# Experts in threes of 32 slots, with 32 slots more that a TensorE register assigns, and weights in tiles of three places

## The chip, the cores and the metric

The kernel runs on one core of one Trainium2 chip. The metric is the device time of one execution in microseconds (us); shorter is better.

## The reference

Two networks run one after the other on 256 tokens of 1024 numbers in float32. The first mixes tokens, attends to a memory and has a dense feed-forward part. The second has two layers, each a token mixer and then a mixture of 32 experts, both steered by numbers (`mod`) computed from a condition `c` with the weights `w_ada`. Only the mixture is touched by the change:

```python
for layer in range(DEPTH_2):
    mod = c_act @ w_ada[layer] + b_ada[layer]
    sh_mix, sc_mix, g_mix, sh_ffn, sc_ffn, g_ffn = jnp.split(mod[:, None, :], 6, axis=-1)
    ...
    x = x + (g_mix * mixed).astype(x.dtype)
    h = (rmsnorm(x, norm_ffn_g[layer]) * (1.0 + sc_ffn) + sh_ffn).astype(x.dtype)
    moe = hierarchical_moe(h, ...)
    x = x + (g_ffn * moe).astype(x.dtype)
...
# in hierarchical_moe: 4 groups of 8 experts; the best group, and in it the best 2
weights = jax.nn.softmax(top_logit, axis=-1) * p_grp
expert_id = g_idx[:, None] * EXPERTS_PER_GROUP + top_idx
combine = ...
hid = jax.nn.silu(jnp.einsum('td,edf->tef', t, w_gate[sl])) * jnp.einsum('td,edf->tef', t, w_up[sl])
y = y + jnp.einsum('tef,efd->td', hid * combine[:, sl, None], w_down[sl])
```

A token uses 2 of the 32 experts. An expert has gate and up weights of 1024 x 256 and down weights of 256 x 1024, 1 MiB each, so a layer's experts hold 96 MiB. Counted from the reference's inputs, no expert of layer 0 has more than 25 tokens; in layer 1 expert 5 has 35 and all others at most 26.

## The kernel before

Everything is kept on the chip except the weights, which stream in through one queue: SyncE issues every weight transfer in program order, and a transfer waits there until its place is free. A place is 8 KB a partition and takes one tile `w` of 128 x 2048 numbers, 1 MiB. The places come from pools (`wst` 5, `wst2` 2, `wst3` 5, later 3, `wst4` 3); `load_w` (L208 in the profile) takes the next place in turn. Matrix products outside the experts split both operands in two parts and take three products (`mm3`, L261 to L263).

The `ada` weights are used by a filler: its tiles (L1031) and matmuls (L1033, four groups of 32 columns that write to different partitions of a bank) are put among other work. Behind each third of a layer's `mod`, four transposes (L1045) bring it into columns.

A mixture begins when the mixer's last residual sum is made (L1188 multiplies by the gate row, L1189 adds). Then come the norm, transposes (`to_T`, L362), router logits (L1631), `route` (L1520 to L1567), which gives each token's rank within its expert (`rankm`) and its weight (`comb`), and the main loop of 16 steps `j` of two experts with 64 slots each:

- `group(G)`, once for two steps: one-hot matrices `Sg` of tokens by slots (L1655), and with them the gather by matmul (L1667), which gives the slots' transposed activations `XT`; the slots' weights `cslot` (L1682).
- `gate(j)` and `up(j)`: `pair_mm` (L1574), eight slices of 128 of the 1024 inputs, each with a matmul of 64 columns for the one expert and one for the other.
- `mid(j)`: transposes of the product into `hd`, and of `Sg` into `ST` (L1706, L1709, copies at L1712, L1714).
- `down(j)`: L1723, output 512 wide, scaled and split into `oh`, `ol` (L1729 to L1731).
- `scatter(j)`: L1738 and L1739 add the slots back to tokens in four banks `yb`.

A float32 matmul shows as two records on TensorE, a transpose as one. TensorE's order in the loop is written by hand: gate j, down j-1, up j, scatter j-1, a piece of gather, mid j, a piece of gather. The weights arrive in the order gate j, down j-1, up j (`ExpertLoads`, seven pairs asked for ahead). Gate and up tiles are read with row k x 128 + p on partition p, so their runs in memory are 1 KB; the down tiles' are 4 KB, and ada's 8 KB. If an expert had more than 64 tokens, a branch (`overflow`) would compute the rest; with these inputs it doesn't run.

Of the kernel before, what the change touches and what calls it, by code (L numbers as in the profile page):

```python
# [9 lines left out]
F32 = mybir.dt.float32  # L10
F32R = mybir.dt.float32r
# [14 lines left out]
for _name, _w in (("g_mix_pre", 8), ("conv_w", 16), ("conv_b", 4), ("lru_b_a", 4), ("lru_b_x", 4),  # L26
# [67 lines left out]
def _params(a):  # L94
# [9 lines left out]
    for name in ("g_mix_pre", "conv_w", "conv_b", "lru_b_a", "lru_b_x", "lru_a_param", "pool_scale",  # L104
                 "b_gate", "g_mem_pre", "g_mem_kv", "g_ffn_pre", "norm_mix_g_2", "norm_ffn_g_2",
                 "conv_w_2", "conv_b_2", "ssd_norm_g_2", "hgrn_norm_g_2", "hgrn_lower_bounds_2", "c_2", "b_ada_2"):
        put(name, cols(a[name]))
    put("ssd_d_2", cols(np.repeat(a["ssd_d_2"], 64, axis=1)))
# [23 lines left out]
class Net:  # L132
# [4 lines left out]
    def __init__(self, ctx, tc, A, out, dbg=None, stop=None):  # L137
# [3 lines left out]
        self.cap = 64  # L141
# [46 lines left out]
    def wtile(self):  # L188

        place = self.places.pop(0)  # L190
        self.places.append(place)
        return place[0].tile([P, 2048], F32, name="w", tag=place[1])

# [10 lines left out]
    def load_w(self, src, k, n):  # L204

        t = self.wtile()
        v = t[:, :k * n].rearrange("p (k n) -> p k n", k=k)
        self.nc.sync.dma_start(v, src.rearrange("(k p) n -> p k n", p=P))  # L208
        return v
# [194 lines left out]
    def build(self):  # L404
# [4 lines left out]
        self.kept = [self.more_places(ctx, "wst", 5)]  # L409
# [51 lines left out]
    def mixer1(self, ph):  # L461
# [121 lines left out]
        self.kept.append(self.more_places(self.ctx, "wst2", 2))  # L583
# [426 lines left out]
    def ada(self):  # L1010
# [9 lines left out]
        for l in range(2):  # L1020
# [6 lines left out]
            for g in range(3):  # L1027
# [16 lines left out]
                for c in range(4):  # L1044
# [3 lines left out]
                                cols(self.V["b_ada_2"], l * 48), op=OP.add)  # L1048
                self.ready = 3 * l + g
# [18 lines left out]
    def mixer2(self, l):  # L1068
# [5 lines left out]
        with c:  # L1074
# [435 lines left out]
    def route(self, l, pr, lg, comb, rankm, cnt):  # L1510
# [24 lines left out]
        o2, M = T("o2", 32), T("Mx", 32)  # L1535
        for tt in range(2):
            v.tensor_scalar(o2[:, tt], iota[:, :32], ei[:, tt, 1:2], None, op0=OP.is_equal)
        for tt in range(2):
            v.scalar_tensor_tensor(M[:, tt], iota[:, :32], ei[:, tt, 0:1], o2[:, tt], op0=OP.is_equal, op1=OP.add)
        bk = self.bank()  # L1540
        te.matmul(bk[:, 0:64], C["before"], M.rearrange("p t e -> p (t e)"), start=True, stop=False)
        te.matmul(bk[:, 32:64], C["ones"], M[:, 0], start=False, stop=True)
        v.scalar_tensor_tensor(rankm, bk[:, 0:64].rearrange("p (t e) -> p t e", t=2), 1.0, M, op0=OP.add, op1=OP.mult)
        v.tensor_scalar(rankm, rankm, -1.0, None, op0=OP.add)
# [6 lines left out]
        w1, w2 = T("w1", 1), T("w2", 1)  # L1551
# [6 lines left out]
        for tt in range(2):  # L1558
            v.tensor_scalar(t[:, tt], iota[:, :32], ei[:, tt, 0:1], w1[:, tt], op0=OP.is_equal, op1=OP.mult)
# [304 lines left out]
```

## Time and profile before

| | |
|---|---|
| median of 3 runs | 1407.7 us (1407.28 to 1409.37) |
| profiled execution | 1404.32 us, span 1402.5 us |
| TensorE matmuls busy | 1320.0 us, 94% of the span |
| VectorE, ScalarE busy | 731.3 us (52%), 571.7 us (41%) |
| weight queue (q1) | 367.84 MB, 77.3% of 16 engines' span |
| mean granted clock | 0.980 |

The span runs from the first to the last instruction of the one execution that was profiled; the profiled execution's own time is a little longer than its span. A busy share is a mean over stages: the experts of the two layers take about 709 to 959 and 1143 to 1391 us of the span.

### The profile page before, as it was taken

How to read it: one execution, taken by the hardware profiler on the slowest of the kernel's cores; microseconds unless marked ns; L12 is line 12 of the kernel's file. 1: busy time of each engine (PE TensorE's matmuls, PEld its weight loads, DVE VectorE, ACT ScalarE, POOL GpSimd, SP SyncE). 2: the span in 40 equal slices, each digit the busy share in tenths (PEclk: the TensorE clock that was granted, in tenths of full speed). 3: DMA queues.
4: the chain of work that ended last, by engine and by line, in shares of the span. 5: the costliest groups of instructions: out<-in, count | busy, mean ns of one | idle time of the engine just before them, and what ended most of it. 6: DMA issues, size and time to landing. Idle time of an engine off the chain costs nothing. (4 is left out here: it accounts for less than half of the span.)

```text
span 1402.5 us, 23768 instructions
## 1 busy us (share of the span) xinstructions
PE 1320.0 (94%) x9842; PEld 1040.5 (74%) x9842; DVE 731.3 (52%) x1350; ACT 571.7 (41%) x1056; POOL 86.1 (6%) x95
## 2 busy tenths in 40 slices
PE   7999999999999998999799999988999989999995
PEld 7988898966999976888666666556888666666652
DVE  5797656536555546865533333326766543333323
ACT  5577546545444435465322222215455322222122
POOL 2000000000000002211100000002121110000000
PEclk9998999999999999999899999998999979999998
DMA  9542559689965539653799999998663499999995
GB/s 309 176 158 92 165 180 317 239 342 366 327 189 200 182 128 327 209 181 121 280 310 366 366 366 366 366 373 305 211 211 121 153 331 366 366 366 367 367 366 188
DMA packets 254817, 375.75 MB, mean 268 GB/s; under 512 B 7057, under 2 KB 221201, under 8 KB 248305
## 3 DMA queue, kind: packets, MB, share of 16 engines
q1 hardware_dynamic: 252960, 367.84, 77.3%
q0 software_dynamic: 1312, 5.21, 1.1%
q8 instruction: 79, 1.29, 0.4%
q10 hardware_dynamic: 432, 1.13, 0.2%
q14 instruction: 34, 0.27, 0.1%
HBM read 373.11 MB, written 1.05 MB: 267 GB/s over the span
## 5 line engine op out<-in xcount | busy, mean ns | idle before, releaser
L225 DVE TENSOR_TENSOR wlo<-w,whi 128x1024 fp32r<-128x1024 f32 x214 | 263.0, 1231 | 181.4 <-ACT whi L223 181.0
L223 ACT ACTIVATE whi<-w 128x1024 fp32r<-128x1024 f32 x214 | 226.4, 1060 | 254.4 <-PE bk L262 171.2
L261 PE MATMUL bk<-hTh,whi 128*128 128x256 f32 (+1 forms) x1128 | 321.0, 287 | 0.8 <-ACT whi L223 0.7
L262 PE MATMUL bk<-hTl,whi 128*128 128x256 f32 (+1 forms) x1128 | 316.4, 281 | 2.1 <-DVE hTl L368 1.9
L263 PE MATMUL bk<-hTh,wlo 128*128 128x256 f32 (+1 forms) x1128 | 315.3, 281 | 0.1
L1574 PE MATMUL bk<-w,XT 128*64 128x256 f32 x2048 | 238.5, 381 | 13.3 <-DMA w<-in_w_up 13.3
L261 PEld LDWEIGHTS bk<-hTh,whi 128*128 128x128 f32 (+1 forms) x1128 | 210.9, 188 | 15.2 <-issue 4.1
L1574 PEld LDWEIGHTS bk<-w,XT 128*64 128x64 f32 x2048 | 146.2, 137 | 100.2 <-DMA w<-in_w_up 16.9
L262 PEld LDWEIGHTS bk<-hTl,whi 128*128 128x128 f32 (+1 forms) x1128 | 210.2, 186 | 4.8 <-DVE hTl L368 2.5
L263 PEld LDWEIGHTS bk<-hTh,wlo 128*128 128x128 f32 (+1 forms) x1128 | 210.0, 186 | 0.7 <-DVE wlo L225 0.3
L1723 PE MATMUL bk<-w,hd 128*64 128x512 f32 x512 | 117.5, 593 | 2.1 <-DMA w<-in_w_down 1.2
L1730 ACT ACTIVATE oh<-od 128x512 fp32r<-128x512 f32 x64 | 40.3, 629 | 116.4 <-DVE od L1729 116.4
L1723 PEld LDWEIGHTS bk<-w,hd 128*64 128x64 f32 x512 | 36.9, 137 | 63.3 <-issue 54.8
L1712 ACT ACTIVATE hd<-bk 128x256 f32<-128x256 f32 x32 | 12.3, 385 | 174.1 <-PE bk L1709 174.1
L1675 DVE TENSOR_SCALAR XT<-bk,ga,modcol 128x256 f32<-128x256 f32 x64 | 34.8, 544 | 85.0 <-PE bk L1667 81.8
L1695 DVE SCALAR_TENSOR_TENSOR mth<-mth,bk 128x256 f32<-128x256 f32 x32 | 13.5, 421 | 118.8 <-ACT mth L1694 118.8
L1731 DVE TENSOR_TENSOR ol<-od,oh 128x512 fp32r<-128x512 f32 x64 | 44.3, 692 | 46.8 <-ACT oh L1730 46.6
L1667 PE MATMUL bk<-Sg,xh 128*128 128x256 f32 x256 | 66.8, 294 | 1.3 <-DVE Sg L1655 1.3
L1667 PE MATMUL bk<-Sg,xl 128*128 128x256 f32 x256 | 64.3, 286 | 0.0
L1729 DVE TENSOR_TENSOR od<-bk,gb 128x512 f32<-128x512 f32 x64 | 44.0, 688 | 37.7 <-PE bk L1723 37.7
L1738 PE MATMUL yb<-oh,ST 128*128 128x512 f32 x128 | 54.4, 425 | 1.6 <-ACT oh L1730 1.6
L1667 PEld LDWEIGHTS bk<-Sg,xh 128*128 128x128 f32 x256 | 49.5, 194 | 4.6 <-issue 2.0
(496 smaller groups left out, 2056.8 us busy)
## 6 DMA issues: line engine op xcount, KB each, us to landing
w<-in_w_gate SPq DMA_DIRECT2D x64, 1024.0 KB, 12.0
w<-in_w_up SPq DMA_DIRECT2D x64, 1024.0 KB, 13.2
w<-in_w_down SPq DMA_DIRECT2D x64, 1024.0 KB, 11.2
w<-in_w_in SPq DMA_DIRECT2D x48, 1024.0 KB, 6.2
w<-in_w_ada SPq DMA_DIRECT2D x48, 1024.0 KB, 5.1
w<-in_w_ffn_in SPq DMA_DIRECT2D x22, 1024.0 KB, 11.5
w<-in_w_out SPq DMA_DIRECT2D x12, 1024.0 KB, 5.1
w<-in_w_ffn_out SPq DMA_DIRECT2D x11, 1024.0 KB, 10.1
```

Source lines behind the costliest of these rows:

```text
L223: self.nc.scalar.activation(W.hi, v, AF.Copy)
L225: self.nc.vector.tensor_tensor(W.lo, v, W.hi, op=OP.subtract)
L261: mm(out, l.hi, r.hi, start=start, stop=False)
L262: mm(out, l.hi, r.lo, start=False, stop=False)
L263: mm(out, l.lo, r.hi, start=False, stop=stop)
L1574: self.nc.tensor.matmul(out[i * 64:i * 64 + 64, :S], XT[:, k, c0:c0 + 64], w[i][:, k, :], start=k == 0, stop=k == KT - 1)
L1667: te.matmul(o, xx[:, tt, d * P:(d + 1) * P], Sg[:, tt].rearrange("p e r -> p (e r)"), start=n == 0, stop=n == 3)
L1723: te.matmul(bks[h][i * 64:i * 64 + 64, :], hd[:, f, i * 64:i * 64 + 64], wd[i][:, f, h * 512:h * 512 + 512], start=f == 0, stop=f == 1)
L1729: v.tensor_tensor(t, bks[h], self.gb[:, h * 512:h * 512 + 512], op=OP.mult)
L1730: act.activation(o.hi, t, AF.Copy)
L1731: v.tensor_tensor(o.lo, t, o.hi, op=OP.subtract)
L1738: te.matmul(yb[tt][h], ST[:, tt * P:(tt + 1) * P], os[h].hi, start=j == 0, stop=False)
```

## The change

The experts are taken in threes, in eleven steps (the last has two). A step has 128 slots in four groups of 32: groups 1 to 3 belong to the three experts, and group 0 to the first of the three that was chosen more than 32 times, for its tokens from rank 32 on. Which one that is is known only at run time: `route` writes eleven indices to `idx`, they are loaded to TensorE's registers ahead of the loop (L1825), and group 0's matmul reads the third of the weight tile that the register names. `slots_mm` (L1621) takes the place of `pair_mm`: four matmuls of 32 columns for each slice. The branch for overfull experts now acts on what is left above 32, or 64 for the expert with the spare slots; with these inputs it doesn't run.

All expert tiles are read with rows p x 8 + k (down: p x 2 + f) on partition p, which makes each partition's part one run of 8 KB; the columns of `XT` and of the transposed product are permuted to fit, by strided copies into `xh`, `xl` and by a permuted copy of `mod` and of the norm's factors. That copy is made by sixteen matmuls with one column behind the transposes of the second and third part of each layer's `mod` (L1073).

The weights' places are now a ring of five tiles with three places each, 15 MiB as before. The ring is opened when the mixture begins, after the places of before are closed (`self.top`, `self.wctx`); layer 0 closes it again and opens the old places for the mixer of layer 1.

```diff
-    def load_w(self, src, k, n):
+    def load_w(self, src, k, n, rows="(k p)"):
...
+                if g:
+                    bk = self.bank()
+                    twin = row.rearrange("p (i k) -> p k i", k=8)
+                    for k in range(8):
+                        for h in range(2):
+                            q = (2, 0)[g - 1] + h
+                            te.matmul(bk[h * 64:h * 64 + 64, k:k + 1], twin[:, k], self.ident[:, q * 32:q * 32 + 1],
+                                      start=True, stop=True)
...
-            old, self.places = self.places, []
-            self.more_places(self.top, "wst3", 3)
-            self.places[:0] = old
...
+        v.tensor_scalar(over, count, 32.0, None, op0=OP.is_gt)
+        v.tensor_copy(sel[:, :, 0], over[:, :, 0])
+        v.tensor_tensor(sel[:, :, 1], over[:, :, 1], over[:, :, 0], op=OP.is_gt)
+        v.tensor_tensor(both, over[:, :, 0], over[:, :, 1], op=OP.max)
+        v.tensor_tensor(sel[:, :, 2], over[:, :, 2], both, op=OP.is_gt)
+        v.scalar_tensor_tensor(idx[:, :11], sel[:, :, 2], 2.0, sel[:, :, 1], op0=OP.mult, op1=OP.add)
...
         for k in range(KT):
-            for i in range(2):
-                c0 = j * P + i * 64
-                self.nc.tensor.matmul(out[i * 64:i * 64 + 64, :S], XT[:, k, c0:c0 + 64], w[i][:, k, :],
+            for i in range(4):
+                c0 = j * P + i * 32
+                wi = w[i]
+                self.nc.tensor.matmul(out[i * 32:i * 32 + 32, :S], XT[:, k, c0:c0 + 32], wi[:, k * S:(k + 1) * S],
                                       start=k == 0, stop=k == KT - 1)
...
-                k, n = (2, D) if name == "w_down_2" else (KT, S)
-                self.ready.append([self.net.load_w(self.net.A[name][self.l, 2 * j + i], k, n) for i in range(2)])
+                t = self.net.wtiles(True)
+                for i in range(min(3, 32 - 3 * j)):
+                    self.net.nc.sync.dma_start(t[:, i], self.net.A[name][self.l, 3 * j + i].rearrange("(p k) n -> p (k n)", p=P))
+                self.ready.append(t)
...
+            self.top.close()
+            self.wctx.close()
+            rp = (c, self.ctx)[l].enter_context(tc.tile_pool(name="ring", bufs=1, side="right", reuse_waits="tile"))
+            self.ring = [(rp, "t%d" % i) for i in range(5)]
...
+            def weights(j):
+                w = loads.get()
+                return [w[:, bass.ds(ats[j], 1)].rearrange("p o n -> p (o n)")] + [w[:, i] for i in (0, 1, min(2, 31 - 3 * j))]
...
+            _, ats = nc.values_load_multi_w_load_instructions(
+                idx[0:1, :11], engines=[mybir.EngineType.PE], min_val=0, max_val=2,
+                skip_runtime_bounds_check_because="idx is 2 a + b of two flags of which at most one is set")
```

Two places show how instructions move. The first is SyncE's queue where layer 0's mixture begins. Before, expert tiles stand among the mixer's output weights and ahead of three of the four ada tiles:

```order
L208 DMA w<-in_w_out 128x2x1024 [waits DMAHW3_49,DVE_49]
L1031 DMA w<-in_w_ada 128x2048 [waits DMAHW4_49,DVE_49]
L208 DMA w<-in_w_out 128x2x1024 [waits PE_49,Pool_49]
L208 DMA w<-in_w_gate 128x8x256 [waits DMAHW5_49,DVE_49]
L208 DMA w<-in_w_out 128x2x1024 [waits DMAHW6_49,PE_49]
L208 DMA w<-in_w_gate 128x8x256 [waits DMAHW7_49,DVE_49]
L208 DMA w<-in_w_up 128x8x256 [waits DMAHW0_49,DVE_49]
L208 DMA w<-in_w_up 128x8x256 [waits DMAHW1_49,DVE_49]
L208 DMA w<-in_w_gate 128x8x256 [waits DMAHW2_49,DVE_49]
L208 DMA w<-in_w_gate 128x8x256 [waits DMAHW6_49,DMAHW3_49,DVE_49]
L208 DMA w<-in_w_down 128x2x1024 [waits DMAHW4_49,DVE_49]
L208 DMA w<-in_w_down 128x2x1024 [waits DMAHW5_49,DVE_49]
```

Behind the change the same place reads:

```order
L223 DMA w<-in_w_out 128x2x1024 [waits DMAHW3_49,DVE_49]
L223 DMA w<-in_w_out 128x2x1024 [waits DVE_49,PE_49,Pool_49]
L223 DMA w<-in_w_out 128x2x1024 [waits DMAHW4_49,PE_49]
L1048 DMA w<-in_w_ada 128x2048 [waits DMASW4_49,DMASW5_49,DMASW3_49,DMAHW5_49,DVE_49,Activation_49]
L1048 DMA w<-in_w_ada 128x2048 [waits DMAHW6_49]
L1048 DMA w<-in_w_ada 128x2048 [waits DMAHW7_49]
L1048 DMA w<-in_w_ada 128x2048 [waits DMAHW0_49,Activation_49,Pool_49]
L1640 DMA w<-in_w_gate 128x2048 [waits DMAHW3_49,DMAHW4_49,DMAHW1_49,Activation_49]
L1640 DMA w<-in_w_gate 128x2048 [waits DMAHW2_49]
L1640 DMA w<-in_w_gate 128x2048
L1640 DMA w<-in_w_up 128x2048 [waits Activation_49]
```

No expert tile is ahead of the ada tiles any more, and the first ada tile waits on VectorE; the instruction there is the last residual multiply of the mixer (L1217 in the changed kernel). In layer 1 the four ada tiles are issued early as before, and the first gate tile has that wait.

The second place is TensorE's queue where gate 0 begins. Before, with `bk` the bank that a product is written to:

```order
L1682 MATMUL bk<-combS,Sg 128x4 x3
L1574 MATMUL bk<-w,XT 64x256 [waits DMAHW5_49,DVE_49]
L1574 MATMUL bk<-w,XT 64x256
L1574 MATMUL bk<-w,XT 64x256 [waits Activation_49]
L1574 MATMUL bk<-w,XT 64x256
L1574 MATMUL bk<-w,XT 64x256 [waits DVE_49]
```

And behind the change, where the ISA rows are instructions on TensorE's registers:

```order
L1753 MATMUL bk<-combS,Sg 128x8 x3
L1825 TENSOR_LOAD idx [waits DVE_49]
L1621 ISA
L1621 MATMUL bk<-w,XT 32x256 [waits DMAHW2_49,DMAHW3_49,DMAHW1_49,DVE_49]
L1621 MATMUL bk<-w,XT 32x256 x3
L1621 ISA
L1621 MATMUL bk<-w,XT 32x256 [waits Activation_49]
L1621 MATMUL bk<-w,XT 32x256 x3
```

Pairs of matmuls have become fours with one register instruction ahead of each; gate and up have sixteen of them in a step and down four. The load of the indices stands ahead of gate 0.

## Rows read from the trace of the kernel before

**Rows 1.** Windows: each engine's busy time, granted clock, DMA share, GB/s

```profile
1150.00:1375.00 225.00, 220.02 (x1591) 141.24 (x1592) 72.52 (x141) 47.83 (x102) 0.00 (x0) 1.00 1.07 366
```

**Rows 2.** Timeline of SyncE: start, length from first to last, issues of up tiles

```profile
738.02 6.69 SPq L208 DMA_DIRECT2D w<-in_w_up  x2
...
927.97 6.47 SPq L208 DMA_DIRECT2D w<-in_w_up  x2
```

**Rows 3.** Timeline of TensorE in mid-stage: start, length, line, operation, count

```profile
823.82 3.67 PE L1574 MATMUL bk<-w,XT 128*64 128x256 f32 x32
827.32 3.60 PE L1723 MATMUL bk<-w,hd 128*64 128x512 f32 x16
...
838.64 3.67 PE L1574 MATMUL bk<-w,XT 128*64 128x256 f32 x32
```

**Rows 4.** Timeline of TensorE at the two layers' ends, idle time before in brackets

```profile
944.01 3.67 PE L1574 MATMUL bk<-w,XT 128*64 128x256 f32 x30 [2.29 <-DMA w<-in_w_up]
...
950.55 3.65 PE L1723 MATMUL bk<-w,hd 128*64 128x512 f32 x16 [0.47 <-ACT hd L1712]
...
1377.96 3.67 PE L1574 MATMUL bk<-w,XT 128*64 128x256 f32 x30 [2.29 <-DMA w<-in_w_up]
...
1384.51 2.80 PE L1723 MATMUL bk<-w,hd 128*64 128x512 f32 x12 [0.47 <-ACT hd L1712]
```

**Rows 5.** Transfers at 298 to 302, 692 to 696, 702 to 703 us; the page's ada issues

```profile
DMA packets 228, 1.70 MB, mean 426 GB/s; under 512 B 20, under 2 KB 20, under 8 KB 20
...
w<-in_w_ada SPq DMA_DIRECT2D x3, 1024.0 KB, 13.9
...
DMA packets 1378, 1.39 MB, mean 348 GB/s; under 512 B 17, under 2 KB 1378, under 8 KB 1378
...
w<-in_w_gate SPq DMA_DIRECT2D x1, 1024.0 KB, 9.9
...
DMA packets 100, 0.41 MB, mean 414 GB/s; under 512 B 0, under 2 KB 0, under 8 KB 99
...
w<-in_w_ada SPq DMA_DIRECT2D x48, 1024.0 KB, 5.1
```

**Rows 6.** Timeline of TensorE: ada's quads, and a set in 64-column groups

```profile
522.36 7.07 PE L1033 MATMUL ada<-w,cact 128*32 128x512 f32 x64 [0.63 <-ACT bk L333]
...
1068.20 1.09 PE L1227 MATMUL bk<-con,rs 128*64 128x128 f32 x16
```

**Rows 7.** Lines L1774 and L1775: register work, ns min/median/max, by queue

```profile
L1774 SPq FUSED_REGOPS  x2: 164/168/173, 939.4 to 1373.9; - x2
...
L1774 PEldq TENSOR_LOAD <-cnt x2: 310/400/491, 956.8 to 1390.7; - x2
...
L1775 SPq EVENT_SEMAPHORE  x6: 17/17/17, 952.8 to 1374.5; - x6
...
L1775 PEldq EVENT_SEMAPHORE  x2: 51/51/51, 959.2 to 1392.2; - x2
```

**Rows 8.** Timeline of SyncE and VectorE where the two mixtures begin

```profile
668.10 8.85 SPq L208 DMA_DIRECT2D w<-in_w_down  x2
...
682.98 0.69 DVE L1188 TENSOR_TENSOR junk<-ob,gb 128x512 f32<-128x512 f32 x1
...
1098.77 8.85 SPq L208 DMA_DIRECT2D w<-in_w_down  x2
...
1113.67 0.69 DVE L1188 TENSOR_TENSOR junk<-ob,gb 128x512 f32<-128x512 f32 x1
```

**Rows 9.** Timeline of TensorE: gate 0 of layer 1

```profile
1142.84 2.38 PE L1574 MATMUL bk<-w,XT 128*64 128x256 f32 x20
```

**Rows 10.** The low clock: a window, and the transposes behind a wait

```profile
688.00:691.00 3.00, 3.00 (x18) 2.83 (x21) 2.04 (x4) 1.60 (x3) 0.00 (x0) 0.55 1.02 360
...
687.09 3.46 PE L362 MATMUL bk<-con,n5xn 128*128 128x128 f32 x16 [3.61 <-DVE n5xn L347]
```

**Rows 11.** Line L1045: the transposes of `mod`, four in each of six sets, first and last start

```profile
L1045 PE MATMUL bk<-con,modrow x24: 272/273/328, 298.6 to 1118.9; 128*128 128x128 f32 x24
```

More of the change, by code (lines that the diff above doesn't have):

```diff
@@ L107, in _params @@
         put(name, cols(a[name]))
+    put("norm_ffn_p", a["norm_ffn_g_2"].reshape(2, P, 8).transpose(1, 0, 2).reshape(P, 16))
+    o = PCOLS["b_ada_2"][0]
+    for l in range(2):
+        for i, c in ((3, 16), (4, 40)):
+            v[:, o + l * 48 + c:o + l * 48 + c + 8] = a["b_ada_2"][l, i * D:(i + 1) * D].reshape(P, 8)
     put("ssd_d_2", cols(np.repeat(a["ssd_d_2"], 64, axis=1)))
@@ L188, in wtile @@
     def wtile(self):
+        if self.ring:
+            self.rest = self.rest or self.wtiles()
+            return self.rest.pop(0)
         place = self.places.pop(0)
@@ L192, in wtile, with wtiles @@
         return place[0].tile([P, 2048], F32, name="w", tag=place[1])
+    def wtiles(self, whole=False):
+        self.ring.append(self.ring.pop(0))
+        t = self.ring[-1][0].tile([P, 3, 2048], F32, name="w", tag=self.ring[-1][1])
+        return t if whole else [t[:, i] for i in range(3)]
     def more_places(self, ctx, name, n):
@@ L408, in build @@
         self.places = []
-        self.kept = [self.more_places(ctx, "wst", 5)]
+        self.ring, self.rest = [], []
+        self.wctx = ctx.enter_context(ExitStack())
+        self.kept = [self.more_places(self.wctx, "wst", 5)]
         self.per = pool("per", 1)
@@ L1540, in route @@
         bk = self.bank()
[L1541 to L1544, printed above, removed]
+        for tt in range(2):
+            te.matmul(bk[:, 66:99], C["ones"], M[:, tt], start=tt == 0, stop=tt == 1)
@@ new lines, in route @@
+        te.matmul(bk[:, 0:66], C["before"], M.rearrange("p t e -> p (t e)"), start=True, stop=False)
+        te.matmul(bk[:, 33:66], C["ones"], M[:, 0], start=False, stop=True)
+        three = lambda t: t.rearrange("p (j i) -> p j i", i=3)
+        count = three(bk[:, 66:99])
+        over, both = pr.tile([P, 11, 3], F32, name="over"), pr.tile([P, 11], F32, name="both")
+        v.tensor_scalar(over, count, 32.0, None, op0=OP.is_gt)
+        v.tensor_copy(sel[:, :, 0], over[:, :, 0])
+        v.tensor_tensor(sel[:, :, 1], over[:, :, 1], over[:, :, 0], op=OP.is_gt)
@@ new lines, in route @@
+        v.tensor_scalar(rank[:, :, :, 1:], mr, -1.0, None, op0=OP.add)
+        v.tensor_tensor(rs, mr, sel.unsqueeze(1).to_broadcast([P, 2, 11, 3]), op=OP.mult)
+        v.tensor_reduce(r1, rs, axis=AX.X, op=OP.add)
+        v.tensor_scalar(rank[:, :, :, 0], r1, -33.0, None, op0=OP.add)
+        mc = pr.tile([P, 1], F32, name="mc")
+        v.scalar_tensor_tensor(over, sel, -32.0, count, op0=OP.mult, op1=OP.add)
+        v.tensor_reduce(mc, over, axis=AX.XY, op=OP.max)
+        v.tensor_copy(idx[:, 11:12], mc)
@@ L1715, in mid, with down @@
                 return hd, ST
-            def down(hd):
-                wd = loads.get()
+            def down(j, hd):
+                wds = weights(j)
                 bks = [self.bank(), self.bank()]
@@ L1738, in scatter @@
                         te.matmul(yb[tt][h], ST[:, tt * P:(tt + 1) * P], os[h].hi, start=j == 0, stop=False)
-                        te.matmul(yb[tt][h], ST[:, tt * P:(tt + 1) * P], os[h].lo, start=False, stop=j == 15)
+                        te.matmul(yb[tt][h], ST[:, tt * P:(tt + 1) * P], os[h].lo, start=False, stop=j == 10)
             def pieces():
-                for G in range(1, 8):
+                for G in range(1, 6):
                     yield from group(G)
@@ L1792, in overflow @@
         with tc.For_i(0, 32, 1) as e:
-            hT, wg, wu, wd = [self.wtile() for _ in range(4)]
+            hT, wg, wu, wd, th = [self.wtile() for _ in range(5)]
+            self.rest = []
             hT = hT.rearrange("p (k t) -> p k t", k=KT)
```

173 lines of the change are left out of this document (100 added, 73 removed), and 2 rows, old and new, of the table _n.

## The prediction

> **What bounds the kernel now.** I read the windows by stage first. In the stretch in which layer 1's experts run (layer 0's looks the same), TensorE is busy for 220.02 of 225 us at full clock, but the DMA queues are busy too (share 1.07) and move 366 GB/s [rows 1]. So two resources look full, and the view of single transfers has to say which of them sets the pace.
>
> The issue rows do. SyncE issues a pair of up tiles at 738.02 and the pair eleven steps later at 927.97 [rows 2]: 17.27 us a step, in which six tiles of 1.0486 MB pass (364 GB/s). TensorE repeats its step every 14.82 us, from gate row to gate row, with 3.60 to 3.67 us each for gate, down and up and the rest (about 3.9) for scatter, gather and transposes [rows 3]. TensorE starts with a stock of tiles, eats it up, and at the end waits 2.29 us for up weights in both layers, to begin the last down products at 950.55 and 1384.51 [rows 4]. These are the two moments that I forecast. The clock is full there and what follows keeps its length, so moving them moves the end.
>
> What limits the transfers? The view of transfers has three short stretches with one sort of tile in flight: ada weights, 8 KB a run, 426 GB/s in 228 packets; gate weights, 1 KB a run, 348 GB/s in 1,378 packets; down weights, 4 KB a run, 414 GB/s [rows 5]. Two thirds of the expert bytes at 348 and one third at 414 give 1/(0.667/348 + 0.333/414) = 367 GB/s, which is the stage's rate. So the length of the runs explains it.
>
> **The change part by part.**
>
> *8 KB runs.* All expert tiles become like the ada tiles: 1.0486 MB / 426 = 2.463 us each instead of 2.865 at 366. A layer has 96: 236.4 us instead of 275.0. Bounds for the rate: 366 (nothing changes) and 426 [rows 1, 5]; I take 426, since shape, size and queue are those of the ada row. The Trainium skill has a rule that speaks against this: "SBUF — State Buffer", Summary, says to count about 358 GB/s, bound by HBM, for HBM to SBUF; by it even the stage of before would have no room, but the 426 of the row is above it on this one core, so the row decides.
>
> *Steps of three.* Eleven steps instead of sixteen, each with nine tiles: 22.2 us of transfers. TensorE's step needs gate and up, 8 quads of four 32-column matmuls each, down (4 quads of 512 columns), scatter, gather, transposes. With q for a gate quad a step takes 16q + 4 × 0.9 + 4.15. A matmul has two records. Ada's quads (512 columns, four groups) come at 64 records in 7.07 us, so 0.88 a quad, and four groups do run together there; sixteen records in 64-column groups take 1.09, so 68 ns each [rows 6]. Pairs take 0.45 now (32 records in 3.62). Bounds for q without the register: 0.45 (array) and 0.88 (eight records at ada's 110 ns); I take 8 × 0.068 = 0.54, as ada's own pace is explained by its 512 columns.
>
> *The register.* Each quad gets one register instruction ahead, 20 a step; the trace of before has none like it on TensorE. Its nearest row is SyncE's register operation, 164 to 173 ns; a semaphore instruction takes 17 ns on SyncE and 51 on TensorE's queue, three times as long [rows 7]. Bounds 0 (it runs ahead of the array) and 0.51 (three times 0.17, nothing overlapped); I take 0.17, so q = 0.71 and the step is 11.4 + 3.6 + 4.15 = 19.1 us, below 22.2. It stays hidden up to q = 0.81 (20.7 us); with its cover gone it is dear, see B. The load of the eleven registers (0.3 to 0.5 us by TensorE's own load of a count, rows 7) stands ahead of gate 0, where weights, not gate 0, set the pace.
>
> *No early tiles.* Before, eight of layer 0's expert tiles are issued ahead of the stage, in single places among the output weights, the last two from 668.10 on; in layer 1 five, the last two from 1098.77 on [rows 8]. After, the ring opens when the old places are empty: the order shows that the first transfer (ada in layer 0, gate in layer 1) waits on VectorE for the last residual multiply, which ends at 683.7 and 1114.4 [rows 8]. I add 2.2 us to the first bytes as an estimate from ada's 5.1 us from issue to landing [rows 5] less its 2.46 of transfer.
>
> Layer 0: 683.7 + 2.2 + 100 tiles × 2.463 = 932.2 for the last landing (four ada, then 96). Behind the last up tile come two down tiles, so up 10 can start at 927.3. It takes up to 5.7 us (8 × 0.71), scatter and transposes 2.4, and the copy of hd with its latency 0.8 to 1.2: down 10 at about 937 instead of 950.55, gain 13.5.
>
> Layer 1: 1114.4 + 2.2 + 236.4 = 1353.0. But the ring's fifteen places are full after 1116.6 + 15 × 2.463 = 1153.6, and the sixteenth needs gate 0 done. Gate 0 ran from 1142.84 [rows 9]; the longer route, one more set of twins and the register load put it 4 to 6 us later, its end near 1152, with the queue's latency 0 to 5 us of stall: I take 2.5. Up 10 then starts at 1350.7, down 10 at about 1361 instead of 1384.51: gain 23.5. In layer 0 the same fill (19 tiles with ada) is over only at 732.7, when gate 0 is long done.
>
> *Clock.* TensorE now waits in each step, and a wait of 3.61 us at 687.09 was followed by three microseconds at 0.55 of the granted clock, thus mostly at the lower of its two levels; the waits of 2.29 us at 944.01 and 1377.96 were not (the 30 records behind them took 3.67) [rows 4, 10]. With work of about 5.7, 3.6 and 9.8 us against tiles landing every 7.4 us, the gaps are 0 to 4 us, so up may sometimes run slow: 3 us at half speed cost 1.5, covered by the 3.1 us that the step has left.
>
> *Twins.* 16 matmuls (32 records) for each of four sets. They go behind four of the six sets of transposes, the first at 298.6 and the last at 1118.9 [rows 11]; three of these lie ahead of the expert stages, where TensorE is the bound, so 3 × 32 × 0.068 = 6.5 us; bounds 0 and 3 × 32 × 0.110 = 10.6. The fourth is in layer 1's start, counted above. The dozen extra VectorE instructions of the route and the strided copies stand before gate 0 too, beside the stream.
>
> Sum: −13.5 − 23.5 + 6.5 = −30.5. On the profiled execution's 1404.32 that is 1374 (span 1372); the median of the runs, 1407.7, lies 3.4 above it, so 1377.
>
> **The rivals.**
>
> A, the stage's 366 is a limit of the memory and not of the runs: the rate stays; the 426 and 414 of rows 5 speak against it. Layer 0's last landing is then 683.7 + 2.2 + 286.5 = 972, later by 40 than in the main case, layer 1 by 38.6: 1377 + 79 = 1456. Equality needs about 399 GB/s.
>
> B, TensorE becomes the bound (the other side): the register instruction is not overlapped and costs more than 0.27 us, or quads come at ada's 0.88. For it: three times slower semaphores on TensorE's queue; against it: 0.17 on SyncE and the 68 ns records. With gate 0 at 711.5 and 1147 the last downs are due after eleven steps p; the two layers equal before at p = 21.65, so with twins the kernel breaks even at p = 21.4, q = 0.85. Beyond that 2 × 11 us for each us of p: q = 0.94 gives p = 22.8 and 1407.7 + 22 × 1.15 + 6.5 = 1439; q = 1.05 some 1479.
>
> C, a part is lost: q between 0.81 and 0.85, or ring stalls (a place of 3 MB comes free only when all of it is used), or the low clock at several waits in a step: 10 to 25 us of the gain go, 1387 to 1403.
>
> D, twins lie beside waits in their stages and the stall in layer 1 is nil: 1368.
>
> E, the longer runs are worth 414, the rate of down now, not 426: 2.533 us a tile, 7 us later in each layer, 1391. The Trainium skill's "DMA: Bandwidth & Descriptors", iDMA fabric, has 408.7 GB/s for a core's stream of rows of 4 KiB; its figure would give 2.566 us and an estimate of 1397. The 8 KB row speaks against both.
>
> **How the numbers follow.** Main case 0.55 (1366 to 1388), D 0.08, C and E 0.18 together, A 0.04, B 0.15. A measurement of this kernel can tell about 0.2% (2.8 us) from no change. Faster by more takes the main case, D and nearly all of C and E: 0.79; near equality 0.03 where C and B meet; slower 0.18. Predicted is the main case, 1377. The range 1364 to 1408 leaves out A, B above equality, and a little below.
>
> **What would show it.** Right: windows in the two stages at 420 GB/s or more with share near 1.0; up-to-up issue every 22 us; TensorE waiting for weights two or three times a step; last downs near 937 and 1361 (less the twins' shift); quads at 0.54 to 0.81 us with weights at hand. Wrong: 366 GB/s with 8 KB packets (A); TensorE without waits and quads above 0.85 (B); gaps in the GB/s slices in mid-stage (C); more than 10 us lost ahead of the expert stages (twins).

## The result and the profile after

The changed kernel takes 1384.44 us (median of 4 runs, 1383.84 to 1385.12) against 1408.53 for the kernel before on the same chip (4 runs, 1407.28 to 1411.5): a ratio of 0.9837, 95% interval 0.9819 to 0.9855, or 24.1 us less. Forecast were 1377 us and 30.5 us less, range 1364 to 1408. The profiled execution took 1384.02 us, its span 1382.1 instead of 1402.5.

Windows of the changed kernel in the two expert stages (columns: window and length, busy time with instructions of PE, PEld, DVE, ACT and POOL, granted clock, DMA share, GB/s), to be read against [rows 1]:

```profile
730.00:920.00 190.00, 143.70 (x1584) 84.00 (x1576) 42.82 (x90) 27.12 (x58) 0.00 (x0) 0.91 1.01 419
1150.00:1340.00 190.00, 151.16 (x1761) 89.47 (x1754) 47.15 (x100) 30.46 (x65) 0.00 (x0) 0.92 1.01 414
1152.00:1160.00 8.00, 8.00 (x128) 5.48 (x123) 1.99 (x4) 1.76 (x5) 0.00 (x0) 1.00 0.82 298
1160.00:1340.00 180.00, 141.16 (x1605) 82.76 (x1598) 44.81 (x93) 28.31 (x60) 0.00 (x0) 0.92 1.01 419
```

The roles have changed. TensorE was busy nearly all the time, and is now idle for a fifth to a quarter of it; the queues are as full as before and move 419 GB/s instead of 366. The 414 of the second row is no slower rate: its window takes in the end of the stall at the ring's opening (298 GB/s from 1152 to 1160), and from 1160 on layer 1 moves 419 as well. The groups of instructions (busy and mean ns of one, idle time ahead and what ended most of it) say for what TensorE waits:

```profile
L1621 PE MATMUL bk<-w,XT 128*32 128x256 f32 (+1 forms) x2816 | 182.7, 418 | 54.9 <-DMA w<-in_w_up 54.6
L1801 PE MATMUL bk<-w,hd 128*32 x704 | 88.5, 647 | 36.7 <-DMA w<-in_w_down 33.7
```

TensorE's timeline at the end of both layers answers to [rows 4] (start, duration, instruction, idle time before):

```profile
941.40 3.66 PE L1621 MATMUL bk<-w,XT 128*32 x64 [1.36 <-DMA w<-in_w_up]
947.93 3.64 PE L1801 MATMUL bk<-w,hd 128*32 x32 [0.47 <-ACT hd L1789]
...
1340.00 6.32 PE L1621 MATMUL bk<-w,XT 128*32 x64 [3.89 <-DMA w<-in_w_up]
...
1357.56 3.64 PE L1621 MATMUL bk<-w,XT 128*32 x64
...
1364.07 3.64 PE L1801 MATMUL bk<-w,hd 128*32 x32 [0.47 <-ACT hd L1789]
```

The last down products begin at 947.93 and 1364.07 instead of 950.55 and 1384.51. In VectorE's timeline the last residual multiplies, which open the mixtures, stand at 689.53 (before 682.98) and 1113.27 (before 1113.67, [rows 8]):

```profile
689.53 0.69 DVE L1217 TENSOR_TENSOR junk<-ob,gb 128x512 f32<-128x512 f32 x1
1113.27 0.69 DVE L1217 TENSOR_TENSOR junk<-ob,gb 128x512 f32<-128x512 f32 x1
```

So the 20.4 us between the spans add up thus: +6.55 ahead of layer 0's mixture, −9.2 in it (258.4 us from residual to last down instead of 267.6), +2.2 between it and the next mixture, −20.0 in layer 1's (250.8 instead of 270.8), 0 behind it. These are two single executions, and the one of the kernel before is a short one (1404.32 us, median 1408.53). The kernel of runs alone, the first experiment below, does the same work up to the experts' loads of layer 0, and there the mixer's transposes stand at 536.05 (before 532.91) and the last residual multiply 4.7 us later than before:

```profile
687.70 0.69 DVE L1188 TENSOR_TENSOR junk<-ob,gb 128x512 f32<-128x512 f32 x1
```

So the first term, 6.55, holds a few us of scatter between executions; the 24.1 us of the medians are the better measure of the whole.

### The profile page after: what moved, and what is told of

It reads as the page before. It is cut to its first block, busy times and chain, and to the rows that moved or that the text cites. A ratio compares the mean times of both kernels' runs of the same rounds, so it can differ in the third digit from the quotient of the medians.

```text
span 1382.1 us, 25644 instructions
## 1 busy us (share of the span) xinstructions
PE 1217.7 (88%) x10662; PEld 958.8 (69%) x10662; DVE 694.3 (50%) x1314; ACT 543.1 (39%) x990; POOL 88.3 (6%) x95
## 5 line engine op out<-in xcount | busy, mean ns | idle before, releaser
L1621 PE MATMUL bk<-w,XT 128*32 128x256 f32 (+1 forms) x2816 | 182.7, 418 | 54.9 <-DMA w<-in_w_up 54.6
L1621 PEld LDWEIGHTS bk<-w,XT 128*32 128x32 f32 x2816 | 102.7, 120 | 133.9 <-issue 72.6
L1801 PE MATMUL bk<-w,hd 128*32 x704 | 88.5, 647 | 36.7 <-DMA w<-in_w_down 33.7
L1801 PEld LDWEIGHTS bk<-w,hd 128*32 128x32 f32 x704 | 26.4, 117 | 88.1 <-issue 85.2
L1807 DVE TENSOR_TENSOR od<-bk,gb 128x512 f32<-128x512 f32 x44 | 30.3, 688 | 72.6 <-PE bk L1801 72.6
L1747 DVE TENSOR_SCALAR XT<-bk,gp,modcol 128x256 f32<-128x256 f32 (+1 forms) x48 | 25.0, 522 | 62.4 <-PE bk L1739 61.1
L1739 PE MATMUL bk<-Sg,xh 128*128 128x256 f32 (+1 forms) x192 | 49.8, 293 | 4.7 <-DVE Sg L1725 4.7
L1050 PE MATMUL ada<-w,cact 128*32 128x512 f32 x384 | 52.9, 667 | 0.6 <-DMA w<-in_w_ada 0.6
L1739 PE MATMUL bk<-Sg,xl 128*128 128x256 f32 (+1 forms) x192 | 48.2, 285 | 0.0
L1809 DVE TENSOR_TENSOR ol<-od,oh 128x512 fp32r<-128x512 f32 x44 | 30.5, 692 | 31.7 <-ACT oh L1808 31.5
```

Of the source, the lines that this page charges most:

```text
L1050: te.matmul(bk[q * 32:(q + 1) * 32, :], cact[:, k:k + 1].to_broadcast([P, 32]), w[:, q * 512:(q + 1) * 512], start=k == 0, stop=k == KT - 1)
L1621: self.nc.tensor.matmul(out[i * 32:i * 32 + 32, :S], XT[:, k, c0:c0 + 32], wi[:, k * S:(k + 1) * S], start=k == 0, stop=k == KT - 1)
L1739: te.matmul(o, xx[:, tt, d * P:(d + 1) * P], Sg[:, tt, :nj].rearrange("p j s -> p (j s)"), start=m == 0, stop=m == 3)
L1801: te.matmul(bks[h][ps, :], hd[:, f, ps], wds[i][:, f * D + h * 512:f * D + h * 512 + 512], start=f == 0, stop=f == 1)
L1807: v.tensor_tensor(t, bks[h], self.gb[:, h * 512:h * 512 + 512], op=OP.mult)
L1809: v.tensor_tensor(o.lo, t, o.hi, op=OP.subtract)
```

## The experiments

My theory: the length of the runs set the rate; transfers bound the new kernel's stages and hide TensorE's steps and registers; the twins ahead of the first mixture, and the lost early tiles, eat part of the gain. The rivals: the gain comes from the steps of three (less TensorE work) and not from the runs; the register costs time; the twins lie beside waits and cost nothing.

**Runs alone.** Pairs of 64 slots as before, but every expert tile read in 8 KB runs; the activations are not permuted to fit.

```diff
-    self.net.load_w(self.net.A[name][self.l, 2 * j + i], k, n)
+    self.net.load_w(self.net.A[name][self.l, 2 * j + i], k, n, "(p k)")
```

> The kernel before with only the expert tiles' runs lengthened to 8 KB; steps of two, places and early tiles as before. It leaves out the permutation of the activations that would fit the rows, so its products pair wrong rows. Theory (run length sets the transfer rate, and TensorE's step of 14.8 us then becomes the bound): the expert stages move data at 415 to 426 GB/s whenever places are free, the waits of TensorE for weights (13.3 + 1.2 us in the kernel before) go, so 1394 us, 1389 to 1399. Rival (fewer, larger steps give the gain and the runs matter little): the stages stay near 366 GB/s and the time within 3 us of 1408.

Measured: 1387.9 us, ratio 0.9841 (0.9819 to 0.9864), better than I expected. Its windows and TensorE's last down products:

```profile
740.00:900.00 160.00, 160.00 (x1174) 102.88 (x1171) 54.73 (x106) 34.88 (x73) 0.00 (x0) 1.00 1.01 418
```
```profile
944.78 3.65 PE L1723 MATMUL bk<-w,hd 128*64 128x512 f32 x16 [0.47 <-ACT hd L1712]
1367.93 3.65 PE L1723 MATMUL bk<-w,hd 128*64 128x512 f32 x16 [0.47 <-ACT hd L1712]
```

418 GB/s without any step of three, and TensorE now without a gap: it is the bound. From the start of gate 0 (713.85 and 1137.00) to the last down both layers take 230.93 us, equal to 0.01. The queues are as full, for six tiles of 2.5 us take 15.0 us a step against TensorE's 14.8; but by the trace's landings the last down weights are there 18 us before the last down products begin. Against the kernel before on its chip (1408.23) 20.3 us are had by this alone, without what the permutation costs.

**Steps of three with the old runs.** The changed kernel with gate, up and down tiles read in 1 and 4 KB runs; the activations stay permuted.

```diff
-    self.net.nc.sync.dma_start(t[:, i], ....rearrange("(p k) n -> p (k n)", p=P))
+    k = 2 if name == "w_down_2" else KT
+    self.net.nc.sync.dma_start(t[:, i].rearrange("p (k n) -> p k n", k=k), ....rearrange("(k p) n -> p k n", p=P))
```

> The changed kernel with gate and up tiles read in 1 KB runs and down tiles in 4 KB runs, everything else as changed; it leaves the activations permuted for the other layout, so its products pair wrong rows. Theory: 366 GB/s in the stages, 2.865 us a tile instead of the 2.503 that the changed kernel shows, 96 x 0.36 = 35 us later in each layer: 1454 us, 1445 to 1460. Rival (steps of three with their fewer TensorE pieces carry the gain): below 1408.

Measured: 1457.16 us, ratio 1.0353 (1.0331 to 1.0374), with these windows in the two layers:

```profile
740.00:930.00 190.00, 131.71 (x1364) 74.17 (x1364) 40.26 (x84) 24.48 (x51) 0.00 (x0) 0.87 1.07 365
1200.00:1370.00 170.00, 124.91 (x1320) 72.47 (x1312) 37.58 (x80) 23.22 (x49) 0.00 (x0) 0.86 1.07 367
```

The old rate is back and TensorE idles more; 1457 is also the time that the prediction gave for a rate of 366 (rival A, 1456). So the rate follows the runs, and with the old runs the rest of the change makes the kernel 48.9 us slower than before (1408.23 on this chip): it leaves out early tiles and adds twins, and what it saves on TensorE lies in waits for weights.

**No twins.** The twin matmuls are left out and the expert activations are scaled with the unpermuted columns, so that part of the computation is not the reference's.

```diff
-    twin = row.rearrange("p (i k) -> p k i", k=8)
-    ... (sixteen matmuls, one addition)
-    bp = mod[:, 16:24]
+    bp = mod[:, 24:32]
```

> The changed kernel without the sixteen one-column matmuls behind the transposes of mod; it takes the columns in the old order, so it leaves out the permutation of mod and of the norm's factor. Theory (they lie on TensorE's path): the last residual multiply of layer 0 ends near 683.7 again instead of 690.2, the second layer starts 2 us sooner on top, and gate 0 of layer 1 comes 2 to 4 us sooner: 9 to 13 us less, 1371 to 1376 us. Rival (the 6.5 us ahead of layer 0's mixture come from the places and early tiles taken away): that time stays at 689 to 691 and the gain is at most 4 us.

Measured: 1376.33 us, ratio 0.9771 (0.9748 to 0.9793), 8.1 us below the changed kernel. The price is paid at a place that TensorE's timeline shows, in the changed kernel first:

```profile
525.34 2.09 PE L1073 MATMUL bk<-con,modrow 128*64 128x1 f32 x32 [0.64 <-ACT bk L348]
527.36 9.88 PE L1050 MATMUL ada<-w,cact 128*32 128x512 f32 x64
539.61 1.97 PE L377 MATMUL bk<-con,n4xn 128*128 128x128 f32 x16
```

and in this kernel:

```profile
521.50 8.77 PE L1050 MATMUL ada<-w,cact 128*32 128x512 f32 x64 [0.63 <-ACT bk L348]
532.63 1.97 PE L377 MATMUL bk<-con,n4xn 128*128 128x128 f32 x16
```

A set takes 2.09 us, two sets stand ahead of layer 0's mixer, and the ada products behind the second take 9.88 us, against 8.77 without twins; in the kernel before they took 7.07 [rows 6], so a part of the slowness isn't the twins'. In the window behind the set the granted clock was 0.50:

```profile
527.50:531.00 3.50, 3.50 (x20) 0.85 (x21) 1.90 (x5) 2.00 (x5) 1.40 (x2) 0.50 0.15 26
```

The mixer's transposes come 7.0 us earlier without twins, of which 5.0 are left at layer 0's last residual multiply (684.49 instead of 689.53). The third set costs about half a us only; the fourth lies ahead of layer 1's gate 0 (36.2 us behind the residual, 31.3 without twins).

**No register.** Group 0 always takes the first expert of the three, and the load of the indices is gone; overflow tokens of the other experts then use wrong weights.

```diff
-    return [w[:, bass.ds(ats[j], 1)].rearrange("p o n -> p (o n)")] + [w[:, i] for i in (0, 1, min(2, 31 - 3 * j))]
+    return [w[:, i] for i in (0, 0, 1, min(2, 31 - 3 * j))]
```

> The changed kernel with group 0 of every step reading the first expert's weights by a fixed address: no register instruction, no load of indices; it leaves out the choice of the expert that gets the spare slots. Theory (TensorE waits for weights in every step, so the 51 ns a quad are hidden): within 2.8 us of the changed kernel's 1384.4, at best 1.5 us less by the load of the indices ahead of gate 0. Rival (the register instructions hold TensorE back): 5 us less or more, and quads shorter than 0.457 us.

Measured: 1384.49 us, ratio 0.9838 (0.9813 to 0.9863): no difference to the changed kernel. In the changed kernel's trace the register instructions (count, ns min/median/max, first and last start) are

```profile
L1621 PEldq FUSED_REGOPS  x352: 51/55/60, 718.0 to 1359.3; - x176
```

that is 55 ns, a third of SyncE's in [rows 7], and all hidden.

**One ring tile fewer in layer 1, or in layer 0.** Four tiles instead of five in one layer.

```diff
-    self.ring = [(rp, "t%d" % i) for i in range(5)]
+    self.ring = [(rp, "t%d" % i) for i in range(5 - l)]
```

> The changed kernel, computing the same, with four ring tiles (twelve places) instead of five in layer 1 only. Theory (in layer 1 the ring is full before gate 0 has begun, and the transfers then stand until gate 0 is done at about 1153): twelve places are full three tiles sooner, the stream stands some 7.5 us longer, 1390 to 1393 us. Rival (layer 1's time is that of its bytes alone; four tiles are enough to keep the queue fed): within 2.8 us of 1384.4.

Measured: 1391.67 us, ratio 0.9919 (0.9896 to 0.9941), as expected. SyncE's issues, in the changed kernel

```profile
1114.11 1.35 SPq L1640 DMA_DIRECT2D w<-in_w_gate  x3
...
1130.57 5.27 SPq L1640 DMA_DIRECT2D w<-in_w_up  x3
1153.21 1.98 SPq L1640 DMA_DIRECT2D w<-in_w_gate  x3
```

and with four tiles

```profile
1120.95 6.69 SPq L1640 DMA_DIRECT2D w<-in_w_down  x3
1152.79 1.28 SPq L1640 DMA_DIRECT2D w<-in_w_up  x3
```

With five tiles the ring is full behind up 1 and SyncE stands until gate 0 gives a tile back at 1153.21; with four this begins a tile earlier, and layer 1's stage is 5.8 us longer. SyncE's wait isn't the queue's: tiles asked for are still arriving. In the changed kernel only the 8 us from 1152 to 1160 are slow, at 298 instead of 419 GB/s, which is 2.3 us lost; with four tiles the 12 us from 1144 to 1156 run at 100 and lose 9:

```profile
1144.00:1156.00 12.00, 12.00 (x161) 9.08 (x160) 3.13 (x9) 2.64 (x5) 0.00 (x0) 0.87 0.28 100
```

The stall at the ring's opening is real. With `range(4 + l)` the same was done to layer 0:

> The changed kernel, computing the same, with four ring tiles instead of five in layer 0 only. Theory (layer 0's transfers begin so late that gate 0 is done before the ring is full; the ring's size matters only where it fills up): within 2.8 us of 1384.4, against the 7 us that the same edit cost in layer 1. Rival (a ring of four is too small to keep the queue fed in mid-stage, and that was the cost in layer 1): 5 us slower or more.

Measured: 1381.6 us, ratio 0.9823 (0.9801 to 0.9846). The stage got shorter, by 4.5 us, against what I had reckoned: four tiles don't reach into the memory of the gate row `gb`, which the last residual multiply reads, so the first ada tile is issued at 682.34 and not at 690.28:

```profile
682.34 2.08 SPq L1048 DMA_DIRECT2D w<-in_w_ada  x4
```

The first byte came 7.9 us earlier, and only 4.5 were gained, for now the smaller ring fills up in layer 0 too: SyncE stands until ada gives its tiles back at 713.08, and the queues nearly stop:

```profile
709.00:714.00 5.00, 4.76 (x24) 2.38 (x24) 3.45 (x28) 0.00 (x0) 0.00 (x0) 0.50 0.08 31
```

So both count in layer 0 as well, the first byte and the room behind it.

**Tiles issued early.** In layer 0, three ring tiles that lie in free memory are filled with gate 0, up 0 and gate 1 during the mixer's end; ada gets the other two.

```diff
+    t = [self.wtiles(True) for _ in range(5)]
+    self.ring = [self.ring[i] for i in (0, 1, 4, 2, 3)]
+    self.given = [t[4], t[2], t[3]]
+    loads = self.ExpertLoads(self, l, 3)
+    self.rest = [t[i // 3][:, i % 3] for i in range(6)]
```

> The changed kernel, computing the same, with the first three ring tiles of layer 0 (nine places) put where weights of the mixer are used up early, and asked for ahead of the four ada tiles, which get the places that come free last. Theory (layer 0's stage is paced by its transfers from the first byte on, so transfers that start sooner end it sooner): the expert tiles are issued from about 655 to 685 us instead of behind the ada tiles at 690.3, nine tiles of 2.5 us are off the stream, less a few us in which the fuller ring waits for gate 0 (718): 15 to 22 us less than the changed kernel, 1363 to 1369. Rival (the first gate product, not the first byte, sets the stage, as in the kernel before): within 3 us of 1384.4.

Measured: 1398.51 us, ratio 0.9955 (0.9939 to 0.9971). I had missed a wait. SyncE's and TensorE's timelines:

```profile
656.43 1.29 SPq L1640 DMA_DIRECT2D w<-in_w_gate  x3
691.78 1.77 SPq L1048 DMA_DIRECT2D w<-in_w_ada  x4
737.34 1.28 SPq L1640 DMA_DIRECT2D w<-in_w_down  x3
```
```profile
735.37 2.78 PE L1050 MATMUL ada<-w,cact 128*32 128x512 f32 x24
```

The early issues worked, but down 0 needs a tile that ada holds, and ada's products stand behind gate 1 in TensorE's order. From 705 to 737 the queues move next to nothing:

```profile
705.00:737.00 32.00, 23.45 (x280) 17.46 (x284) 14.49 (x60) 5.18 (x12) 2.45 (x1) 0.78 0.01 3
```

**The permuted `mod` by DMA.** Instead of the twins, two small transfers on ScalarE's queue write a column tile `modp`; the router reads permuted rows, and the transposes of these thirds go.

```diff
-    ... (transposes and twins)
+    mp = self.per.tile([P, 8], F32, name="modp")
+    for h in range(2):
+        nc.scalar.dma_start(mp[h * 64:h * 64 + 64], row[(q + h) * 32:(q + h) * 32 + 1].rearrange("o (p k) -> o p k", k=8))
```

> The changed kernel, computing the same, with the permuted columns of mod brought by two small transfers from the row (ScalarE's queue) in place of the sixteen matmuls; the router too works on permuted rows, so that the old transposes of the second and third part go as well. Theory (the one-column matmuls cost the 8 us that their removal gave): 1374 to 1378 us; a little less than 1376.3, as four transposes a set go too. Rival (the small transfers are late, or hold ScalarE's queue): 1380 or more, with TensorE or VectorE waiting for them.

Measured: 1378.45 us, ratio 0.9811 (0.9793 to 0.9829). Nearly all of the twins' price ahead of layer 0 is back (transposes at 533.91), but in layer 1 VectorE waits 8.33 us for `modp`, on the path to the router:

```profile
1122.24 0.17 DVE L1072 TENSOR_TENSOR modcol<-modp,par 128x8 f32<-128x8 f32 x1 [8.33 <-DMA modp<-modrow]
```

and gate 0 stands 39.9 us behind the residual (36.2 in the changed kernel). Both this and the early tiles in one kernel:

> Both of the two changes above in one kernel, computing the same as the reference. Theory: they act in different places and add: 1384.4 - 18 - 9 = 1357 us, 1352 to 1363. Rival (the fuller ring only waits longer for gate 0): 1365 or more.

Measured: 1390.19 us, ratio 0.9891 (0.9875 to 0.9906): the same hole as with the early tiles, 2 GB/s from 700 to 729 (layer 0's stage 270.4 us), and SyncE's wait ends with ada's products again, not with gate 0 as the rival had it.

**Ada early.** To mend that, ada goes first into the two free tiles, and the experts' first three into the others; the twins are replaced by transfers on ScalarE's queue as above, the transposes kept.

```diff
+    self.ring = [self.ring[i] for i in (4, 2, 3, 0, 1)]
+    self.given = [t[3], t[0], t[1]]
+    self.rest = [t[(4, 2)[i // 3]][:, i % 3] for i in range(6)]
+    self.fill(FILL["moe"])
```

> The changed kernel, computing the same, with the permuted columns of mod brought by two small transfers (the old transposes and the router's rows stay) and, in layer 0, the ring entered the other way: the four ada tiles go to the tiles whose memory comes free first (issued from about 655), gate 0 to the third of them, up 0 and gate 1 to the two that come free with the last residual sum. Theory (the early start failed in the run before because the two tiles with ada were given back only after gate 1; here ada's products come before gate 0): 1376 less 9 to 14 us for four ada and some expert tiles off the stream, 1362 to 1367 us, with a gap of a few us ahead of down 0. Rival (the stage follows gate 0 and not the first byte): 1374 to 1378.

Measured: 1381.8 us, ratio 0.9820 (0.9801 to 0.9838), a miss by 15. Ada is issued at 652.20, but SyncE's third issue of gate 1 stands until 716.7:

```profile
690.43 26.30 SPq L1634 DMA_DIRECT2D w<-in_w_gate  x3
```
```profile
705.00:717.00 12.00, 9.83 (x45) 6.75 (x46) 8.26 (x48) 1.65 (x4) 0.00 (x0) 0.51 0.02 2
```

The view of SyncE's waits (us in total, times, longest) names the small `modp` transfer as what ended this one:

```profile
SPq L1634 <- DMA modp<-modrow: 25.1, 1, 25.1
```

That transfer itself waits for ada's products. So a transfer on another engine's queue held the weights. I put it down to a completion semaphore that the two share in the program; no run changed the semaphore alone.

**Pairs with the right permutation.** Runs alone, with the activations and `mod` permuted to fit: strided copies, and `modp` by transfers on ScalarE's queue.

```diff
+    act.activation(split(xh[:, tt]), perm(xn[:, tt]), AF.Copy)
...
+    act.activation(XT[:, d], o, AF.Identity, scale=gp[:, d:d + 1], bias=bp[:, d:d + 1])
```

> The kernel before, computing the same, with 8 KB runs for the expert tiles, the activations permuted to fit, and mod's permuted columns brought by two small transfers; steps of two, 64 slots, single places. Theory (8 KB runs give most of the change's gain, and with steps of two TensorE's 14.8 us a step set the pace): 1386 to 1393 us, TensorE waiting for no weights. Rival (the permuted layout itself costs what the runs bring): 1400 or more.

Measured: 1400.31 us, ratio 0.9939 (0.9922 to 0.9957), a miss by 7 to 14. VectorE's timeline shows the `modp` wait ahead of the copies that the router needs:

```profile
1125.90 0.17 DVE L1061 TENSOR_TENSOR modcol<-modp,par 128x8 f32<-128x8 f32 x1 [6.49 <-DMA modp<-modrow]
```

Where TensorE is the bound, what comes ahead of gate 0 moves the end: gate 0 is 35.84 us behind layer 1's residual, 29.18 in the kernel of runs alone. So pairs that compute the reference gain 7.4 us by the long runs, not 20.3, while the changed kernel, also with the permutation, gains 24.1.

**Both mended.** Ada early as above, but `modp` goes over GpSimd's queue and its additions stand behind the route, where nothing on the router's path waits for them.

```diff
-    nc.scalar.dma_start(mp[h * 64:h * 64 + 64], ...)
-    v.tensor_tensor(self.mod[l][:, o:o + 8], mp, ...)
+    nc.gpsimd.dma_start(mp[h * 64:h * 64 + 64], ...)
...
+    with tc.issue_after(getattr(end, "ins", end)):
+        ... (the two additions and gp)
```

> The changed kernel, computing the same, entered as in the run with ada first (ada to the tiles that come free first), and with mod's permuted columns brought by small transfers on GpSimd's queue, whose completions no weight transfer waits for, and added on VectorE only behind the route. Theory (the run with ada first was held at gate 1, whose third tile waited until 716.7 for the completion of a small transfer on the shared semaphores; and the small transfers on VectorE's way to the router kept gate 0 of layer 1 back by 2 to 4 us): gate 1's tiles leave without a gap, layer 0's stage from last residual sum to last down takes 248 to 251 us instead of 258.4, the ways of the mixers are as without the sixteen matmuls: 1366 us, 1361 to 1371. Rival (the early transfers only move the wait to the ring): 1374 or more.

Measured: 1368.86 us (1366.63 to 1370.17), ratio 0.972 (0.9703 to 0.9737): 15.6 us below the changed kernel and the fastest of all. Gate 1 leaves without a gap and down 0 at 708.32. The hole shrinks but isn't gone: from 705 to 717 the queues move 245 GB/s, where the kernel with ada early moved 2. The last down products come at 933.94 and 1348.73:

```profile
650.30 21.51 SPq L1048 DMA_DIRECT2D w<-in_w_ada  x4
...
688.55 1.40 SPq L1633 DMA_DIRECT2D w<-in_w_gate  x3
708.32 1.28 SPq L1633 DMA_DIRECT2D w<-in_w_down  x3
```
```profile
705.00:717.00 12.00, 11.27 (x63) 8.17 (x66) 7.37 (x36) 2.58 (x5) 1.09 (x2) 0.58 0.62 245
```
```profile
933.94 3.64 PE L1805 MATMUL bk<-w,hd 128*32 x32 [0.47 <-ACT hd L1793]
1348.73 3.64 PE L1805 MATMUL bk<-w,hd 128*32 x32 [0.47 <-ACT hd L1793]
```

## Why the prediction was right, and where its sizes were off

The mechanism was right: the runs set the rate, the transfers bound the stages, and TensorE's steps are hidden. The sum was 10 us too good in the profiles (−30.5 against −20.4) and 6.4 in the medians (24.1 us gained). That each stage is off by only 4 us is in part luck, for two errors stand against each other. Behind its residual multiply the last up begins 7.5 us later than forecast in layer 0 (251.9, forecast 244.3) and 7.3 later in layer 1 (244.3, forecast 237.0); from there to the last down it takes 6.5 us in both, 3.2 and 3.8 less than forecast. The stages are thus 4.3 and 3.5 longer (258.4, forecast 254.1; 250.8, forecast 247.3).

- *8 KB runs.* The mis-sized term, and the 7 us. 426 GB/s came from a window of 4 us with 1.70 MB of ada tiles [rows 5]. Over 190 us the experts run at 419, so 2.503 us a tile and not 2.463, or 3.9 us over the tiles up to the last up. The rest is mostly gaps: by the trace's landings the tiles come 2.49 us apart, but three times in either layer 3.7 to 4.0, and with these layer 0's mean is 2.54, which is 7.4 us over 97 tiles. One such gap, at 817.7, shows in SyncE's issues too, where three take 6.49 us instead of 5.3:

```profile
806.37 5.26 SPq L1640 DMA_DIRECT2D w<-in_w_up  x3
813.85 6.49 SPq L1640 DMA_DIRECT2D w<-in_w_gate  x3
822.59 5.35 SPq L1640 DMA_DIRECT2D w<-in_w_down  x3
```

  What makes the gaps is open. Most of the step from 426 to 419 is the short window: the same ada stretch of the kernel before gives 422 over 12 us, and six windows of 4 us from 760 to 784 in the changed kernel lie between 410 and 424.

```profile
296.00:308.00 12.00, 11.28 (x70) 6.69 (x69) 1.72 (x4) 2.88 (x5) 0.00 (x0) 1.00 1.01 422
```

  Rival A (the memory limits at 366) is out by the 419 and by the short-run kernel. E (414, 1391) is as near to the result as the main case, and its 2.533 us a tile nearer to the 2.54 of the landings than my 2.463; its reason, the rate of the old down tiles, isn't what the windows show (419). The Trainium skill's "HBM Reference", Specifications (TRN2), lets a core that streams alone reach about 425 GB/s; the 419 of this single core agrees with it, and not with the 358 of the page that I had set against the row.
- *Steps of three and the register.* A quad takes 3.66 / 8 = 0.46 us with its register instruction, not 0.71: the low bound, so a step is some 15 us of TensorE work instead of 19.1. Most of this is hidden, since TensorE waits; the last up (3.66, forecast up to 5.7) makes 2 of the 3 to 4 us by which the way to the last down is shorter. Without the register the time is the same. Rival B is out. But steps of three aren't idle in the gain: with long runs, pairs are held by TensorE, 260.1 us from layer 1's residual to the last down with runs alone, and threes take 250.8 although their gate 0 begins 7 us later behind the residual. Without twins threes take 1376.33 us, pairs 1387.9, neither with the permutation of `mod`. The Trainium skill's "TensorE: Matmul & The Clock Gate", Measured speedup vs the span model, has 2.38 times the pace for three column tiles, less than three; here four groups of 32 take 0.46 us where two of 64 took 0.45 [rows 3]. What one group takes alone no run here shows, so the 2.38 isn't tested.
- *No early tiles.* The first transfers are issued at 690.28 and 1114.11, behind the last residual as forecast, and the stall in layer 1 is there, 2.3 us by the row at 1152 where 2.5 were forecast; the ring runs show both. What early tiles are worth the kernel with both mended shows: layer 0's stage is 247.5 us there, 10.9 less than in the changed kernel.
- *Clock.* I had written that up may sometimes run slow. It does so in 11 of the 22 steps, where it takes 4.97 to 6.55 us instead of 3.66. Behind the wait of 3.89 us at 1340.00 the granted clock was 0.57, so mostly the lower of its two levels:

```profile
1342.00:1346.00 4.00, 4.00 (x48) 2.08 (x40) 0.00 (x0) 0.00 (x0) 0.00 (x0) 0.57 1.01 420
```

  The length of the wait (in brackets) doesn't tell which up is slow:

```profile
900.20 3.66 PE L1621 MATMUL bk<-w,XT 128*32 x64 [3.83 <-DMA w<-in_w_up]
1293.89 5.35 PE L1621 MATMUL bk<-w,XT 128*32 x64 [2.25 <-DMA w<-in_w_up]
```

  The step has room for it, as forecast. At layer 1's end TensorE runs from 1340.00 to the last up at 1357.56 without a wait, but by the landings the last up's weights arrive at 1357.32, so the slow up there costs 0.2 us at most. In the kernel with both mended the last up waits 0.73 us for its weights.
- *Twins.* 6.5 us forecast; the transposes stand 6.7 later than before (539.61, before 532.91). That the two agree is an accident: the same transposes stand at 536.05 with runs alone, without a twin, so as much as 3.1 us of the shift can be scatter. Taking the twins out gives 5.0 us back at layer 0's last residual and some 0.5 for the third set, 5.5 in all where I had counted three sets of 2.2. Without all four the kernel is 8.1 us faster; rival D is out.
- *Not in the sum.* From layer 0's last down to layer 1's last residual 2.2 us more. The mixer of layer 1 takes 153.2 to 153.7 us from its transposes to the residual in the changed kernel and in those without twins and with both mended, and 151.2 in the three pair kernels (before, runs alone, pairs with the permutation). So it isn't the twins. But it isn't the ring alone either: the ring kernels with early tiles, with `modp` by DMA and with both of these take 156.0, 152.8 and 151.3. The cause is open.
- *The signs.* The 1361 named for the second last down leaves out layer 0's gain. With that and the twins' shift the forecast is 943.5 and 1354, and 947.93 and 1364.07 were measured; that 1364 is near 1361 says nothing.

## What to carry to other kernels

When matmuls and transfers both look full, look for a stretch with one sort of tile in flight and compare its rate by run length: making runs longer alone was worth 20 us here. Then ask what holds the kernel next, and what the new layout costs: with the permutation 7.4 of these 20 us were left to the pairs, whose TensorE steps then set the pace, and steps of three brought 24.1. Take the rate of a long stretch, not of 4 us, and count the gaps between landings. When a transfer is moved ahead, follow its buffer to the instruction that gives it back, and every semaphore that the issue waits for: three of four kernels with early tiles opened a hole of 12 to 32 us, while the sound one, with the twins' work moved off the path, gave 15.6.

## What was not expected of the hardware

- A register instruction on TensorE took 51 to 60 ns, a third of SyncE's 164 to 173 [rows 7]; the load of the eleven indices took 1.33 and 1.51 us instead of the 0.31 to 0.49 of single loads, and was hidden.
- The eight small transfers of `modp` by ScalarE's queue (2 KB each, from one tile on the chip to another) took 1.7, 6.2 and 8.4 us (minimum, median, maximum) from issue to landing.
- Two comparisons of 128 x 4 on VectorE, part of the route, took 2.82 us at 703.36 in the changed kernel (0.36 before) while GpSimd ran two permuted subtractions, 5.67 us together from 700.36 on; VectorE's long one ends with the second of these. Layer 1 shows the same at 1132.64. Whether the one slows the other was not tried.
